# A hybrid layer with a streamed mixture of experts: gate chunks and query/key chunks change places, attention steps go between the branch products, the first gather goes between router pieces

## The chip, the cores and the metric

The kernel runs on one core of one Trainium2 chip. The metric is the device time in microseconds from launch to end; lower is better. TensorE (PE) does the matmuls and transposes, VectorE (DVE) and ScalarE (ACT) the elementwise work, SyncE (SP) issues nearly all loads, one after the other, on one queue.

## The reference

```python
def hybrid_layer(x, ...):                      # x: 256 tokens x 1024, float32
    proj = x @ w_in                            # 20 chunks of 256 columns and a low-rank part
    sh = token_shift(proj[..., :SHIFT_COLS], mu_shift)
    y_rwkv = rwkv7_time_mix(...)               # per head and token: state = state*w - (state@kk)(kk*a) + v k; y = state@r
    y_attn = moba_attention(q, k, v)           # rope on q and k; 256 tokens are one block: causal softmax attention
    mixed = (sigmoid(gate_a) * (y_attn @ w_attn_br)
             + sigmoid(gate_r) * (y_rwkv @ w_rwkv_br))
    h = layer_norm(DEEPNORM_ALPHA * x + mixed @ w_out, ln1_g, ln1_b)
    return layer_norm(DEEPNORM_ALPHA * h + moe_ffn(h, ...), ln2_g, ln2_b)

def moe_ffn(x, ...):                           # router: top 4 of 32 experts per token
    # each token's 4 experts: clamped_swiglu(x @ w1[e] + b1[e]) @ w2[e] + b2[e], weighted and added
```

All is float32. A product of the projections, branches and w_out is computed as three fp32r matmuls of a high and a low part (hi·hi, hi·lo, lo·hi): lines L135 to L137 of the kernel.

## The kernel before

The program is written out in one long function, and each engine executes its instructions in the order in which the program makes them, waiting where an operand or a buffer is not ready.

*Projections.* `units()` is a generator: each step of it is one unit, three matmuls. A chunk of 256 columns is 16 units, 320 in all; `fill(n)` draws n units, `fill_to(n)` draws up to the n-th. They stand between the steps of the serial work, so that TensorE has something to do while the other engines work on the step before. Before its units, each chunk has a later chunk's weights cut into high and low parts (`split`: L128 on ScalarE, L129 on VectorE). After its units a chunk is finished: shift chunks on ScalarE and VectorE (L205, L206), query and key chunks by the rotation of `rope` on VectorE (L274, L277, L279), gate chunks by one sigmoid on ScalarE. The order is: shift chunks, values, gate A (4 chunks), queries and keys (4), gate R (4).

*Recurrence.* VectorE makes the operands (L382 to L410), TensorE the products of each of the 4 chunks of 64 tokens (L426), VectorE solves a triangular system (L484, L486), whose blocks go through DRAM. Then comes the chain c = 0..3: L573 (state times keys), L580, L588 (new state), L601 (output) on TensorE, each followed by VectorE (L574, L581, L595/L596, L605) and by a few units. `group_norm(tt)` (L545 to L552) follows every second c, and `group_norm_out(tt)` (transposes L558, then L561, L562) makes the recurrence's result.

*Attention.* Transposes of q and k (L629), then for both halves h of the heads `scores(h)` (L642, L648, softmax L651 to L661), `turn_scores(h)` (transposes L667), `weigh(h)` (L680, L681).

*Branches and out projection.* The two branch products have 4 quarter-chunks of 16 units each; the result, multiplied by the gates G_["R"] and G_["A"], is `mixed`. The out projection takes w_out in 8 rows kt: each is cast (L819, ScalarE) and its low part made (L820, VectorE), then multiplied. The first five rows are done for all of the output, the rest piece by piece, together with the LayerNorm, the transposes L858 and the router L866. w_out arrives in four pieces of 1 MB (`wout_raw` 25 to 28, two rows each).

*Experts.* 32 experts of 12.58 MB each are streamed through twelve 2 MB buffers, whose memory the front uses for other things: `both0` to `both6` are pairs of slots (`BOTH`), the others are q0 to q3 and a pair (11, 13). `mfill(u)` puts the next load into buffer u on SP's queue. In the traces SP's loads of experts are L736, of w_out L758. The first expert starts with L1045 (biases) and L1049. Its rows are gathered by matmuls with one-hot matrices (L912 on VectorE, `gather_rows` L917 on TensorE), for which the router's choice must be known (`route`, `places`).

Of the kernel before, what the change touches and what calls it, by code (L numbers as in the profile page):

```python
# [17 lines left out]
T = 256  # L18
# [44 lines left out]
def hybrid_kernel(ctx, tc, xt_d, x_d, win_d, w0_d, ups_d, up2_d, par_d, cA_d, cB_d, wbr_d, wout_d,  # L63
# [11 lines left out]

    BOTH = [(0, 1), (22, 23), (21, 25), (14, 17), (16, 20), (9, 15), (12, 18)]
    both = [slots.tile([128, 2, 2048], FT, name=f"both{i}", tag=f"both{i}") for i in range(len(BOTH))]
# [27 lines left out]

    chunks = [("low", 0)] + [("in", i) for r in ((0, 6), (10, 16), (6, 10), (16, 20)) for i in range(*r)]
    chunks += [("br", i) for i in (2, 3, 0, 1)]
    raw_of = {0: 25, 21: 10, 22: 8, 23: 16, 24: 20, 25: 12, 26: 18, 27: 12, 28: 18}
    hls = ["q0", "q1", "q3"]
# [141 lines left out]
    def units():  # L251
        yield from proj_shift(1, 0, k, 0, 4)
        yield from proj_shift(2, 1, k, 2, 6)
        yield from proj_shift(3, 0, r, 0, 0)
        yield from proj_shift(4, 1, r, 2, 2)
        yield from proj_shift(5, 0, v, 0, 8)
        yield from proj_shift(6, 1, v, 2, 10)

        for half in range(2):
            yield from proj_tok(7 + half, half,  # L260
                                lambda tt, ps: A.copy(va_tok[:, tt, 256 * half:256 * half + 256], ps))
        G_["A"] = slot(15, [8, T])
        for j in range(4):
            yield from proj_gate(9 + j, j % 2, G_["A"][:, 2 * j:2 * j + 2])
        qk = G_["qk"] = slot(22, [2, 2, 512])
        cosf = cB[:, B_COS:B_COS + 128].rearrange("p (t d) -> p t d", t=2)
        sinf = cB[:, B_SIN:B_SIN + 128].rearrange("p (t two d) -> p t two d", t=2, two=2)
        m1 = s23[:, 1536:1792].rearrange("p (h d) -> p h d", d=64)
        m2 = s23[:, 1792:2048].rearrange("p (h two d) -> p h two d", two=2, d=32)

        def rope(which, half):
            def done(tt, ps):
                pv = ps.rearrange("p (h two d) -> p h two d", two=2, d=32)
                V.tensor_tensor(m1, pv.rearrange("p h two d -> p h (two d)"),  # L274
                                cosf[:, tt, None].to_broadcast([128, 4, 64]), op=OP.mult)
                for x in range(2):
                    V.tensor_tensor(m2[:, :, x], pv[:, :, 1 - x], sinf[:, tt, None, x].to_broadcast([128, 4, 32]),  # L277
                                    op=OP.mult)
                V.tensor_tensor(qk[:, which, tt, 256 * half:256 * half + 256], m1.rearrange("p h d -> p (h d)"),  # L279
                                m2.rearrange("p h two d -> p (h two d)"), op=OP.add)  # L280
            return done

        for u in range(4):
            yield from proj_tok(13 + u, u % 2, rope(*divmod(u, 2)))
        G_["R"] = slot(9, [8, T])
        for j in range(4):
            yield from proj_gate(17 + j, j % 2, G_["R"][:, 2 * j:2 * j + 2])

# [87 lines left out]
    PE.matmul(pd, cA[0:1, A_ONE:A_ONE + 1].to_broadcast([1, 128]), brow, start=False, stop=True)  # L376
    fill_to(46)
    for f2 in range(2):
# [82 lines left out]
    PT = s23[:, 0:1536].rearrange("p (f q) -> p f q", f=4)  # L461
    fill(4)

# [100 lines left out]
    for c in range(4):  # L564
# [56 lines left out]
    V.tensor_tensor(yRs[:, 1], yR, yRs[:, 0].bitcast(FT), op=OP.subtract)  # L621
    fill(8)
    qk = G_["qk"]
    qkT = slot(20, [2, 4, T])
    for f in range(4):
# [4 lines left out]
        A.copy(qkT[:, :, f], ps)  # L630
    fill(4)
    yAs = slot(13, [2, 4, T], FR)
# [4 lines left out]
    def scores(h):  # L637
# [6 lines left out]
        for f2 in range(2):  # L644
            pq = bank((7, 2)[f2], (2, T))
            for ff in range(2):
# [119 lines left out]
    V.tensor_tensor(b1r[:, 1], b1s, b1r[:, 0].bitcast(FT), op=OP.subtract)  # L766
    for n in (25, 26):
        wout_raw(n)
    mfill(0, "q2")
    gA, gR = G_["A"], G_["R"]  # L770
    for br, (ys_, gt) in enumerate(((yRs, gR), (yAs, gA))):
        for cc in range(2):
            n = 21 + 2 * br + cc
            split(n + 2)
            if n == 22:
                xtok = slot(8, [2, D])
                nc.scalar.dma_start(xtok, x_d)
            if n == 23:
                mx = [slot(i, [2, 4, T], FR) for i in (11, 10)]
            for dd in range(2):  # L780
                d2 = 2 * cc + dd
                ps = bank(2 + d2, (2, T))
                for d in range(2):
                    for kt in range(4):
                        c0 = 256 * dd + 128 * d
                        mm3(ps[:, d], [HL[n][:, x, kt, c0:c0 + 128] for x in range(2)], (ys_[:, 0, kt], ys_[:, 1, kt]),
                            kt == 0, kt == 3)
                q = slice(2 * d2, 2 * d2 + 2)
                V.tensor_tensor(gt[:, q], gt[:, q], ps, op=OP.mult)
                if br:  # L790
# [3 lines left out]
                    V.tensor_tensor(m[:, 1, q4], gA[:, q], m[:, 0, q4].bitcast(FT), op=OP.subtract)  # L794
                elif cc == 0 and dd == 0:
                    turn_scores(1)
                elif cc == 0:
                    weigh(1)
                    mfill(3, 1, 2)
# [14 lines left out]
    for kt in range(8):  # L814
# [74 lines left out]


    for n in range(len(todo) + 2):
        if n < len(todo):
            add(*todo[n])
        if n > 1:
            router(*todo[n - 2])
            if n == 3:
                route(0)
        if 0 < n <= len(todo):
            rows_turned(*todo[n - 1])
    route(1)  # L900
    mfill(*[hls[n % 3] for n in (27, 28)])
    dump("lg", lg[:, :, 0:E])

    ext = slot(10, [2048])
    XG, oh = ext[:, 0:1024].rearrange("p (d s) -> p d s", d=8), ext[:, 1024:1280].rearrange("p (t s) -> p t s", t=2)
    rows = ext[32:48, 1280:1408]
    OT = misc.tile([128, 2, 256], FR, name="OT", tag="OT")
# [437 lines left out]
```

## Time and profile before

| | |
|---|---|
| median of 3 runs | 1201.11 us (1199.92 to 1202.76) |
| the profiled execution | 1202.04 us, its span 1200.3 us |
| TensorE busy | 1124.0 us, 94% of the span |
| VectorE, ScalarE busy | 384.2 us, 280.1 us |
| granted TensorE clock, mean | 0.973 of full speed |
| loaded | 441 MB, 367 GB/s over the span |

Times in the views are counted from the start of the span. The execution's own time is 1.7 us more than its span. A busy TensorE is not one at its peak: 64 columns of the array are used in most expert matmuls, and they may wait for weights inside.

### The profile page before, as it was taken

The numbers are of one execution on the slowest core, as the hardware profiler recorded it, in microseconds if no ns is written. First come the engines' busy times: TensorE is split into PE (matmuls) and PEld (weight loads), VectorE is DVE, ScalarE is ACT, GpSimd is POOL, SyncE is SP. The second block draws the span as 40 slices with busy tenths as digits, with TensorE's granted clock in tenths as the row PEclk, the third lists the DMA queues.
The fourth block names the chain that finished last, engine by engine and source line by source line (L and its number), as shares of the span: only waits on it lengthen the run. The fifth ranks groups of instructions, "written<-read, shape, count | busy, mean of one in ns | idle before, by whom it ended". The sixth has DMA issues, their size and how long they took to land. (4 is left out here: it accounts for less than half of the span.)

```text
span 1200.3 us, 15200 instructions
## 1 busy us (share of the span) xinstructions
PE 1124.0 (94%) x6434; PEld 590.3 (49%) x6434; DVE 384.2 (32%) x809; ACT 280.1 (23%) x566; POOL 6.1 (1%) x16
## 2 busy tenths in 40 slices
PE   8989979999999999999999998999999799899995
PEld 6879969985434444343434343433343333343432
DVE  4879576662222222222212121211212111111113
ACT  5634326632111121111111111111111111111112
POOL 0000000000000000000000000000000000000000
PEclk9999989998999999999999999998999899999998
DMA  8344553797999999999999999999999989999995
GB/s 278 127 137 135 152 206 137 324 382 279 428 428 427 428 427 428 427 426 422 426 428 428 428 428 428 428 427 428 427 428 428 420 344 428 427 427 428 428 428 239
DMA packets 45549, 441.02 MB, mean 367 GB/s; under 512 B 13010, under 2 KB 13538, under 8 KB 17954
## 3 DMA queue, kind: packets, MB, share of 16 engines
q1 hardware_dynamic: 36002, 436.93, 87.6%
q10 hardware_dynamic: 9472, 3.05, 1.0%
q8 instruction: 52, 0.85, 0.3%
q14 instruction: 23, 0.19, 0.0%
HBM read 438.13 MB, written 1.84 MB: 367 GB/s over the span
## 5 line engine op out<-in xcount | busy, mean ns | idle before, releaser
L1049 PE MATMUL b<-both,s 128*64 128x512 f32 x1456 | 331.9, 605 | 17.5 <-DMA both<-in_w_dram 17.4
L1049 PEld LDWEIGHTS b<-both,s 128*64 128x64 f32 x1456 | 100.8, 139 | 227.8 <-issue 190.7
L1058 DVE TENSOR_SCALAR s<-b 128x256 f32<-128x256 f32 x64 | 27.2, 424 | 446.9 <-PE b L1049 446.9
L1032 PE MATMUL b<-both,s 128*64 128x512 f32 x624 | 139.7, 595 | 4.0 <-DMA both<-in_w_dram 3.2
L1049 PE MATMUL b<-q,s 128*64 128x512 f32 x576 | 132.4, 606 | 1.6 <-DMA q<-in_w_dram 1.5
L135 PE MATMUL b<-q,q 128*128 128x256 f32 x320 | 96.6, 302 | 0.9 <-ACT q L128 0.9
L1074 ACT COPY s<-b 128x256 f32<-128x256 f32 x64 | 23.7, 370 | 312.0 <-PE b L1069 229.5
L137 PE MATMUL b<-q,q 128*128 128x256 f32 x320 | 92.9, 290 | 0.8 <-DVE q L129 0.8
L136 PE MATMUL b<-q,q 128*128 128x256 f32 x320 | 92.8, 290 | 0.0
L1032 PEld LDWEIGHTS b<-both,s 128*64 128x64 f32 x624 | 43.8, 137 | 86.5 <-issue 82.7
L1032 PE MATMUL b<-q,s 128*64 128x512 f32 x368 | 83.0, 597 | 0.9 <-DMA q<-in_w_dram 0.9
L1022 DVE TENSOR_TENSOR s<-b,s 64x512 fp32r<-64x512 f32 (+1 forms) x66 | 44.3, 672 | 119.2 <-ACT s L1021 117.0
L1021 ACT CAST s<-b 64x512 fp32r<-64x512 f32 (+1 forms) x66 | 37.4, 567 | 189.5 <-PE b L1032 177.8
L1049 PEld LDWEIGHTS b<-q,s 128*64 128x64 f32 x576 | 39.7, 139 | 81.6 <-issue 76.7
L917 PEld LDWEIGHTS b<-s,s 128*128 128x128 f32 x512 | 61.7, 200 | 13.8 <-issue 13.0
L917 PE MATMUL b<-s,s 128*128 128x128 f32 x512 | 65.0, 288 | 1.4 <-DVE rt L961 0.7
L135 PEld LDWEIGHTS b<-q,q 128*128 128x128 f32 x320 | 63.6, 199 | 5.2 <-issue 2.6
L137 PEld LDWEIGHTS b<-q,q 128*128 128x128 f32 x320 | 63.7, 199 | 1.0 <-DVE q L129 1.0
L136 PEld LDWEIGHTS b<-q,q 128*128 128x128 f32 x320 | 63.8, 199 | 0.2 <-issue 0.2
L1059 ACT ACTIVATE s<-s 128x256 f32<-128x256 f32 x64 | 26.9, 421 | 144.7 <-DVE s L1058 144.7
L129 DVE TENSOR_TENSOR q<-both,q 128x1024 fp32r<-128x1024 f32 x44 | 52.4, 1218 | 10.6 <-ACT q L128 10.6
L1045 PE MATMUL b<-b1r,pick 128*128 128x512 f32 x128 | 47.2, 451 | 8.2 <-DVEq L1166 8.2
(291 smaller groups left out, 1040.1 us busy)
## 6 DMA issues: line engine op xcount, KB each, us to landing
both<-in_w_dram SPq DMA_DIRECT2D x130, 2048.0 KB, 25.7
q<-in_w_dram SPq DMA_DIRECT2D x59, 2048.0 KB, 34.5
both<-in_win_dram SPq DMA_DIRECT2D x19, 1024.0 KB, 5.1
both<-in_wout_dram SPq DMA_DIRECT2D x4, 1024.0 KB, 7.0
both<-in_w2l_dram SPq DMA_DIRECT2D x7, 512.0 KB, 21.5
s<-in_wbr_dram SPq DMA_DIRECT2D x2, 1024.0 KB, 6.8
both<-in_wbr_dram SPq DMA_DIRECT2D x2, 1024.0 KB, 4.8
s<-in_w_dram SPq DMA_DIRECT2D x2, 1024.0 KB, 16.5
```

What stands on the lines that cost most here:

```text
L129: V.tensor_tensor(hl[:, 1, c], RAW[n][:, c], hl[:, 0, c].bitcast(FT), op=OP.subtract)
L135: PE.matmul(ps, lhs[0], rhs[0], start=first, stop=False)
L136: PE.matmul(ps, lhs[0], rhs[1], start=False, stop=False)
L137: PE.matmul(ps, lhs[1], rhs[0], start=False, stop=last)
L917: PE.matmul(pg[d // 4][:, d % 4], xtok[:, tt, 128 * d:128 * d + 128], oh[:, tt], start=tt == 0 and d % 4 == 0, stop=tt == 1 and d % 4 == 3)
L1021: A.copy(hi, ps)
L1022: V.tensor_tensor(lo, ps, hi.bitcast(FT), op=OP.subtract)
L1032: PE.matmul(ps[64 * n:64 * n + 64], aTs[e % 2][:, b, hf, 64 * g_:64 * g_ + 64], w[:, hf, 512 * n:512 * n + 512], start=ft == 0, stop=ft == 7)
L1045: PE.matmul(ps, pick, b1r[:, x], start=x == 0, stop=False)
L1049: PE.matmul(ps[64 * g_:64 * g_ + 64], XG[:, kt, 64 * j:64 * j + 64], w[:, kt % 2, 512 * g_:512 * g_ + 512], start=False, stop=kt == 7)
L1058: V.tensor_scalar(gl, pv[:, :, 0], 7.0, None, op0=OP.min)
L1059: A.activation(sw, gl, AF.Sigmoid, scale=1.702)
```

## The change

BOTH is paired anew: pairs 4 and 5 were slots (16, 20) and (9, 15) and are (16, 9) and (20, 15). The chunks' order becomes: gate A (4), gate R (3), queries and keys (4), gate R (the last). Fills change: 46 to 50, 72 to 78, 4 to 9, and in the chain 4 to 5; `group_norm_out(0)` goes behind the chain's last step. The branch products become a generator too, and the steps of attention stand between its units. `wout_raw(26)` goes into the branch, `mfill(5)` from behind piece 28 to ahead of piece 27. In the loop over the router's pieces, the first token half's places, one-hots and gather stand ahead of the last router piece. Lines move: L574, L580, L588 and L601 become L575 and so on, SP's L736 and L758 become L729 and L751, L558 becomes L559, L866 L870, L886/L887 L890/L891, L917 L904.

```diff
-    BOTH = [(0, 1), (22, 23), (21, 25), (14, 17), (16, 20), (9, 15), (12, 18)]
+    BOTH = [(0, 1), (22, 23), (21, 25), (14, 17), (16, 9), (20, 15), (12, 18)]
...
-    chunks = [("low", 0)] + [("in", i) for r in ((0, 6), (10, 16), (6, 10), (16, 20)) for i in range(*r)]
+    chunks = [("low", 0)] + [("in", i) for r in ((0, 6), (10, 19), (6, 10), (19, 20)) for i in range(*r)]
...
+        G_["R"] = slot(20, [8, T])
+        for j in range(3):
+            yield from proj_gate(13 + j, j % 2, G_["R"][:, 2 * j:2 * j + 2])
...
         for u in range(4):
-            yield from proj_tok(13 + u, u % 2, rope(*divmod(u, 2)))
-        G_["R"] = slot(9, [8, T])
-        for j in range(4):
-            yield from proj_gate(17 + j, j % 2, G_["R"][:, 2 * j:2 * j + 2])
+            yield from proj_tok(16 + u, 1 - u % 2, rope(*divmod(u, 2)))
+        yield from proj_gate(20, 1, G_["R"][:, 6:8])
...
-    fill_to(46)
+    fill_to(50)
...
-    fill_to(72)
+    fill_to(78)
...
-    fill(4)
+    fill(9)
...
         if c < 3:
-            fill(4)
-        if c == 2:
-            group_norm_out(0)
-    fill_to(256)
+            fill(5)
+    group_norm_out(0)
+    fill(14)
     group_norm_out(1)
...
-    fill(8)
+    fill_to(312)
...
-    fill(4)
+    fill_to(320)
...
     scores(0)
-    fill(18)
-    scores(1)
-    fill(12)
-    turn_scores(0)
-    fill_to(314)
-    weigh(0)
-    fill_to(320)
...
+    queue = branch(0)
+    fill(16)
+    scores(1)
+    mfill(4)
+    fill(8)
+    wout_raw(26)
+    xtok = slot(8, [2, D])
+    nc.scalar.dma_start(xtok, x_d)
+    turn_scores(0)
+    fill(4)
+    weigh(0)
+    turn_scores(1)
+    fill(2)
+    weigh(1)
+    fill(2)
+    mfill(3, 1, 2)
+    mx = [slot(i, [2, 4, T], FR) for i in (11, 10)]
+    queue = branch(1)
+    fill(32)
     dump("mixT", gA)
-    mfill(4)
+    mfill(5)
...
         if kt in (1, 3):
             wout_raw(27 + kt // 2)
-            if kt == 3:
-                mfill(5)
...
     for n in range(len(todo) + 2):
         if n < len(todo):
             add(*todo[n])
+        if n == len(todo) + 1:
+            pg = [bank(i, (4, 128)) for i in (2, 3)]
+            gather_rows(pg, 0)
         if n > 1:
             router(*todo[n - 2])
             if n == 3:
                 route(0)
+            if n == len(todo):
+                ...
+                places(0)
+                one_hots(0, 0)
         if 0 < n <= len(todo):
             rows_turned(*todo[n - 1])
     route(1)
...
-    places(0)
-    one_hots(0, 0)
-    gather_rows(pg, 0)
     places(1)
```

How the change moves instructions shows best at three places. The first is VectorE in the chain's second and third steps; before, it is this (L274, L277 and L279 are the rotation of a query or key chunk, L129 a chunk's split, L581 to L605 the chain's own):

```order
L574 TENSOR_TENSOR both_71<-b_119_1424,both_71 64x512
L274 TENSOR_TENSOR both_70<-b_111_1313,both_72 128x256
L277 TENSOR_TENSOR both_70<-b_111_1313,both_72 128x4x32 x2
L581 COPY both_73<-b_120_1448 64x512
L279 TENSOR_TENSOR both_70<-both_70 128x256
L129 TENSOR_TENSOR q_121_1458<-both_69,q_121_1458 128x1024
L274 TENSOR_TENSOR both_70<-b_111_1313,both_72 128x256
L277 TENSOR_TENSOR both_70<-b_111_1313,both_72 128x4x32 x2
L129 TENSOR_TENSOR q_121_1458<-both_69,q_121_1458 128x1024
L279 TENSOR_TENSOR both_70<-both_70 128x256
L595 TENSOR_TENSOR s_11_126<-b_124_1474,s_11_126 64x4x64 x2
L596 TENSOR_TENSOR s_11_126<-s_11_126,eC 64x4x64 x2
```

The same place of VectorE's order after the change (L575 is L574 of before, L596 and L597 are L595 and L596):

```order
L575 TENSOR_TENSOR both_71<-b_119_1420,both_71 64x512
L582 COPY both_73<-b_123_1444 64x512
L129 TENSOR_TENSOR q_120_1434<-both_69,q_120_1434 128x1024 x2
L596 TENSOR_TENSOR s_11_126<-b_124_1463,s_11_126 64x4x64 x2
L597 TENSOR_TENSOR s_11_126<-s_11_126,eC 64x4x64 x2
```

The two rotations (six rows) are gone from between the steps; the two splits stay.

The second place is SP's order around the branch's end; `both_74` is pair 5, `in_wout` are pieces 25 to 28 of w_out, in that order. Before:

```order
L736 DMA both_71<-in_w_dram 128x4096
L736 DMA both_73<-in_w_dram 128x4096
L758 DMA both_75<-in_wout_dram 128x2x1024 x2
L736 DMA both_74<-in_w_dram 128x4096
L736 DMA both_75<-in_w_dram 128x4096
```

After:

```order
L729 DMA both_73<-in_w_dram 128x4096
L751 DMA both_75<-in_wout_dram 128x2x1024
L729 DMA both_72<-in_w_dram 128x4096
L729 DMA both_70<-in_w_dram 128x4096
L729 DMA both_71<-in_w_dram 128x4096
L729 DMA both_74<-in_w_dram 128x4096
L751 DMA both_75<-in_wout_dram 128x2x1024 x2
L729 DMA q_202_2438<-in_w_dram 128x4096
L729 DMA both_75<-in_w_dram 128x4096
```

Pair 5 stood behind pieces 27 and 28, and now stands ahead of both.

The third place is TensorE at the end of the router, up to the first expert's biases. Before (L866 is the router, L858 the transposes for it, L917 a gather, L886 and L887 the places of a half):

```order
L866 MATMUL b_206_2448<-wr,zT 128x32 x2
L858 MATMUL b_211_2558<-cA,s_182_2161 128x128 x2
L866 MATMUL b_206_2448<-wr,zT 128x32 x2
L887 MATMUL b_205_2447<-rt,cA 128x32
L917 MATMUL b_215_2582<-s_214_2580,s_182_2161 128x128 x4
L917 MATMUL b_216_2583<-s_214_2580,s_182_2161 128x128 x4
L886 MATMUL b_206_2448<-rt,cA 128x32
L887 MATMUL b_206_2448<-rt,cA 128x32
```

After (L870 is the router, L862 its transposes, L904 the gather, L890 and L891 the places):

```order
L870 MATMUL b_206_2448<-wr,zT 128x32 x2
L891 MATMUL b_205_2447<-rt,cA 128x32
L862 MATMUL b_212_2563<-cA,s_173_2121 128x128 x2
L904 MATMUL b_213_2568<-s_211_2559,s_173_2121 128x128 x4
L904 MATMUL b_214_2569<-s_211_2559,s_173_2121 128x128 x4
L870 MATMUL b_206_2448<-wr,zT 128x32 x2
L890 MATMUL b_206_2448<-rt,cA 128x32
L891 MATMUL b_206_2448<-rt,cA 128x32
```

The first half's gather has moved from behind the last router piece to ahead of it.

## Rows read from the trace of the kernel before

**Rows 1.** Windows: length; busy (instructions) PE, PEld, DVE, ACT, POOL; clock, DMA share, GB/s

```profile
560.00:960.00 400.00, 369.12 (x1828) 150.04 (x1826) 79.42 (x186) 61.04 (x149) 0.00 (x0) 0.97 1.01 427
```

**Rows 2.** TensorE's timeline: start, us, instruction, idle time before it

```profile
273.36 3.78 PE L917 MATMUL b<-s,s 128*128 128x128 f32 x16 [0.61 <-DVE rt L876]
...
278.58 3.65 PE L917 MATMUL b<-s,s 128*128 128x128 f32 x16 [0.75 <-DVE rt L961]
...
282.37 0.73 PE L1045 MATMUL b<-b1r,pick 128*128 128x512 f32 x2
...
314.92 3.84 PE L917 MATMUL b<-s,s 128*128 128x128 f32 x32
```

**Rows 3.** TensorE's waits before 285 us: releaser, us, times, longest

```profile
PE b L558 <- DVE both L552: 3.4, 1, 3.4
PE b L580 <- DVE both L574: 3.1, 1, 3.1
PE b L426 <- DVE s L410: 2.2, 1, 2.2
PE b L468 <- DVE s L206: 1.6, 1, 1.6
PE b L573 <- DVE s L596: 1.5, 1, 1.5
PE b L382 <- DVE both L369: 1.4, 1, 1.4
PE b L558 <- issue: 1.3, 1, 1.3
```

**Rows 4.** Windows of the front, columns as in rows 1

```profile
46.90:54.00 7.10, 7.01 (x38) 6.50 (x39) 6.95 (x14) 2.57 (x6) 0.90 (x2) 0.76 0.09 36
62.20:68.00 5.80, 5.79 (x48) 5.09 (x50) 4.54 (x9) 0.00 (x0) 0.00 (x0) 0.71 0.62 195
...
150.70:159.80 9.10, 7.81 (x86) 7.26 (x87) 7.59 (x16) 4.37 (x6) 0.00 (x0) 1.00 0.23 95
165.40:173.00 7.60, 7.55 (x51) 7.09 (x52) 2.92 (x6) 0.58 (x1) 0.00 (x0) 0.55 0.86 301
178.70:184.00 5.30, 5.30 (x33) 5.30 (x33) 4.15 (x11) 1.05 (x1) 0.00 (x0) 0.68 0.61 198
...
269.10:282.40 13.30, 10.91 (x57) 10.01 (x56) 4.02 (x26) 4.35 (x8) 0.00 (x0) 0.62 0.99 419
```

**Rows 5.** TensorE's timeline: last branch units, the out projection's first and fifth row

```profile
235.77 0.28 PE L137 MATMUL b<-s,q 128*128 128x256 f32 x1
...
243.09 0.40 PE L135 MATMUL b<-q,s 128*128 128x512 f32 x1
...
254.21 0.40 PE L135 MATMUL b<-q,s 128*128 128x512 f32 x1
```

**Rows 6.** VectorE's timeline within the chain

```profile
147.36 1.20 DVE L129 TENSOR_TENSOR q<-both,q 128x1024 fp32r<-128x1024 f32 x1
148.49 0.41 DVE L279 TENSOR_TENSOR both<-both 128x256 f32<-128x256 f32 x1
148.82 0.86 DVE L595 TENSOR_TENSOR s<-b,s 64x256 f32<-64x256 f32 x2
```

**Rows 7.** SP's timeline: issues of pieces 27 and 28 (one row), of pair 5

```profile
235.24 7.91 SPq L758 DMA_DIRECT2D both<-in_wout_dram  x2
246.69 0.34 SPq L736 DMA_DIRECT2D both<-in_w_dram  x1
```

**Rows 8.** DMA issues near 203.6 and 255.8 us: KB, us to landing

```profile
both<-in_w_dram SPq DMA_DIRECT2D x1, 2048.0 KB, 9.3
...
both<-in_w_dram SPq DMA_DIRECT2D x1, 2048.0 KB, 7.5
```

**Rows 9.** ScalarE's timeline: casts of w_out's rows 4 and 5

```profile
249.81 2.00 ACT L819 CAST q<-both 128x1024 fp32r<-128x1024 f32 x2 [3.87 <-DMA both<-in_wout_dram]
```

**Rows 10.** VectorE's timeline: splits of w_out's rows 4 to 7

```profile
250.89 4.86 DVE L820 TENSOR_TENSOR q<-both,q 128x1024 fp32r<-128x1024 f32 x4 [4.23 <-ACT q L819]
```

More of the change, by code (lines that the diff above doesn't have):

```diff
@@ L101, in dump @@
             dbg(name, ap)
-    chunks = [("low", 0)] + [("in", i) for r in ((0, 6), (10, 16), (6, 10), (16, 20)) for i in range(*r)]
+    chunks = [("low", 0)] + [("in", i) for r in ((0, 6), (10, 19), (6, 10), (19, 20)) for i in range(*r)]
     chunks += [("br", i) for i in (2, 3, 0, 1)]
-    raw_of = {0: 25, 21: 10, 22: 8, 23: 16, 24: 20, 25: 12, 26: 18, 27: 12, 28: 18}
+    raw_of = {0: 25, 21: 10, 22: 8, 23: 16, 24: 18, 25: 12, 26: 18, 27: 12, 28: 18}
     hls = ["q0", "q1", "q3"]
@@ L621, in hybrid_kernel @@
     V.tensor_tensor(yRs[:, 1], yR, yRs[:, 0].bitcast(FT), op=OP.subtract)
-    fill(8)
+    fill_to(312)
     qk = G_["qk"]
-    qkT = slot(20, [2, 4, T])
+    qkT = slot(9, [2, 4, T])
     for f in range(4):
@@ L644, in scores @@
         for f2 in range(2):
-            pq = bank((7, 2)[f2], (2, T))
+            pq = bank((7, 0)[f2], (2, T))
             for ff in range(2):
@@ L664, in turn_scores @@
         for i in range(3):
-            ps = bank((6, 7, 2)[i], (4, 128))
+            ps = bank((0, 1, 6)[i], (4, 128))
             for f in range(4):
@@ L766, in hybrid_kernel, with branch @@
     V.tensor_tensor(b1r[:, 1], b1s, b1r[:, 0].bitcast(FT), op=OP.subtract)
-    for n in (25, 26):
-        wout_raw(n)
+    wout_raw(25)
     mfill(0, "q2")
     gA, gR = G_["A"], G_["R"]
-    for br, (ys_, gt) in enumerate(((yRs, gR), (yAs, gA))):
+    def branch(br):
+        ys_, gt = ((yRs, gR), (yAs, gA))[br]
         for cc in range(2):
@@ L774, in hybrid_kernel @@
             split(n + 2)
[L775 to L779, printed above, removed]
             for dd in range(2):
@@ L787, in hybrid_kernel @@
                             kt == 0, kt == 3)
+                        if d + kt < 4:
+                            yield
                 q = slice(2 * d2, 2 * d2 + 2)
@@ L794, in hybrid_kernel @@
                     V.tensor_tensor(m[:, 1, q4], gA[:, q], m[:, 0, q4].bitcast(FT), op=OP.subtract)
[L795 to L799, printed above, removed]
+                yield
+    queue = branch(0)
[17 more added lines that the diff above has]
+    fill(32)
     dump("mixT", gA)
-    mfill(4)
+    mfill(5)
     po = [bank(i) for i in (0, 1, 2, 3, 5)]
@@ L888, in places @@
         V.scalar_tensor_tensor(posm[:, tt], pp, 1.0, sel[:, tt], op0=OP.add, op1=OP.mult)
[L891 to L906, printed above, removed]
     OT = misc.tile([128, 2, 256], FR, name="OT", tag="OT")
@@ L935, in gather @@
         gathered(pg)
-    pg = [bank(i, (4, 128)) for i in (2, 3)]
-    places(0)
-    one_hots(0, 0)
-    gather_rows(pg, 0)
+    for n in range(len(todo) + 2):
+        if n < len(todo):
+            add(*todo[n])
+        if n == len(todo) + 1:
+            pg = [bank(i, (4, 128)) for i in (2, 3)]
+            gather_rows(pg, 0)
+        if n > 1:
+            router(*todo[n - 2])
+            if n == 3:
+                route(0)
+            if n == len(todo):
+                ext = slot(10, [2048])
+                XG, oh = ext[:, 0:1024].rearrange("p (d s) -> p d s", d=8), ext[:, 1024:1280].rearrange("p (t s) -> p t s", t=2)
+                rows = ext[32:48, 1280:1408]
+                places(0)
+                one_hots(0, 0)
+        if 0 < n <= len(todo):
+            rows_turned(*todo[n - 1])
+    route(1)
+    mfill(*[hls[n % 3] for n in (27, 28)])
+    dump("lg", lg[:, :, 0:E])
     places(1)
```

## The prediction

> **What bounds the kernel now.** I read the windows first. From 560 to 960 us the DMA share is 1.01 at 427 GB/s while TensorE is busy 369 of 400 us [rows 1]: the expert stage is paced by its weights. TensorE's timeline then gives the place at which that stage can start, the bias matmul L1045 of the first expert at 282.37 us [rows 2]; 1200.3 - 282.37 = 917.9 us come after it. Twelve 2 MB buffers are filled ahead, and each later load waits until TensorE has read its buffer, so the stream begins when TensorE enters the first expert. I therefore take the end as that entry plus 917.9 us, one for one. None of the change's edits lies behind the entry.
>
> What sets the entry is the front. Its waits on TensorE, listed by engine and releaser, are seven single ones of 1.3 to 3.4 us, and all but one wait for VectorE [rows 3]: L382 for a reciprocal, L426 for L410, L468 for L206, and four in or behind the recurrence's chain (L573, L558 for nothing visible, L580, L558 for L552). Behind most of them the granted clock is below 1 [rows 4]: 0.76 in the 7.1 us from 46.9, 0.71 in the 5.8 from 62.2, 0.55 in the 7.6 from 165.4, 0.68 in the 5.3 from 178.7. A stretch of T us at clock x does the work of T·x at 2.4 GHz, so T·(1-x) is lost: 1.70, 1.68, 3.42 and 1.70 us. TensorE executes the same matmuls before and after up to the last branch product, which ends where the out projection starts, 243.09 us before [rows 5]. So the lead there is idle time removed plus clock loss removed, less what is new.
>
> **The change part by part.** *Fills in the front* (46 to 50, 72 to 78, 4 to 9). A unit is three matmuls at 0.12 us (60 of them lie between 235.77 and 243.09 [rows 5], 7.32/61), so 0.36 us. Four units cover L382's wait of 1.4, six of 2.2 us stand ahead of L426; VectorE gets there about as much earlier as L382 does, so I leave 1.5 of that wait (0 to 2.2). Five units cover L468's 1.6. Removed: 1.4 + 0.7 + 1.6 = 3.7 us, and the clock loss of 1.70 behind 46.9. That behind 62.2 I count as removed and then, since a wait of 1.5 remains there, as kept. New: the six units are missing further on, behind the L426 products; six units are 2.2 us of cover, VectorE is itself earlier, and I take 1.7 (0 to 2.2).
>
> *Gates in place of queries and keys.* In the chain, VectorE's order has a query chunk's rotation and weight split between two updates of the state: L129 for 1.20 us and L279 for 0.41 end at 148.9, where L595 starts (148.82) [rows 6]; TensorE's L573 waits for what follows. A gate chunk ends in a sigmoid on ScalarE, busy for 0.58 of the 7.6 us from 165.4 [rows 4], so this VectorE work leaves the chain; moving group_norm_out(0) behind c = 3 takes L561 and L562 out of it too, and fill(5) adds 0.36 us of cover per step. Removed: 1.5 + 1.3 + 3.1 = 5.9 us of waits and 3.42 of clock loss. What remains of c = 3's latency I charge with 1.0 (0 to 2.2, six units' worth of shift). The rotations fall behind the chain: the second L558 waits for the same kind of work as before (3.4), now with one rotation and two splits ahead of it: 3.6, so 0.2 more (0 to 4), and its 1.70 of clock loss stays.
>
> *Attention between the branch's products.* Between scores(0) and turn_scores(0) there were 30 units, now 16 + 8: 2.2 us less cover for a softmax of unchanged length. I take 1.85 of it as wait, and 0.8 where the first transposes wait for the last rotation: 2.65 (0 to 4).
>
> *Sum at the end of the branch.* Waits 9.6 and clock 1.70 + 1.68 + 3.42 = 6.8 removed: 16.4. New 1.7 + 1.0 + 0.2 + 2.65 = 5.55, clock kept 1.7. Lead 9.15, so the out projection starts at 233.9.
>
> *Buffer pair 5 ahead of w_out's pieces 27 and 28.* This is the part that works against the rest. Before, SP issued piece 27 at 235.24, ahead of the branch's end, and pair 5 only at 246.69, when VectorE had read gate A for the last time: 3.6 us behind the branch's end at 243.09 [rows 5, 7]. Afterwards pair 5 holds the slots of both gates and stands in SP's order ahead of pieces 27 and 28. It still waits for that last read, and both pieces wait behind it. A 2 MB load into an empty or nearly empty queue landed 7.5 to 9.3 us after its issue [rows 8]; 1 MB behind it takes 1.05/427 = 2.45; then ScalarE's cast, 1.0 each [rows 9], and VectorE's split, 4.86/4 = 1.22 each [rows 10]. The fifth row of the out projection would be ready 3.6 + (7.5 to 9.3) + 2.45 + 1.0 + 1.22 = 15.8 to 17.6 us behind the branch's end. TensorE wants it after four rows: 254.21 - 243.09 = 11.1 [rows 5]. Stall 4.7 to 6.4; I take 5.5. ScalarE already waited 3.87 for such a piece before [rows 9], hidden by the rows in hand. Behind 28 the order is slack: a row takes TensorE 2.8, a split 1.22.
>
> The Trainium skill (DMA: Bandwidth & Descriptors, "Anatomy of one DMA") gives 2.0 us fixed and bytes at 436 GB/s. By that page pair 5 would land in an estimated 6.8 us, the stall would be 3.9 and the time about 1196.9. The rows of this case are slower than the page, and the sum goes by them.
>
> *What such a stall does to the clock.* Behind waits of 3.1 and 3.4 us the losses were 3.42 and 1.70 us [rows 3, 4]. Behind 5.5 I take 2.5 (0 to 3.4; 0 because the stretch from 150.7 to 159.8, behind a wait of 1.5, stayed at 1.00 [rows 4]).
>
> *The first gather between the router pieces.* From 269.10 to 282.40 the clock is 0.62, a loss of 5.1 us, and short waits lie in it. The first gather takes 3.78 us from 273.36, the second 3.65 from 278.58, where 32 of the same at 2.4 GHz take 3.84 [rows 2, 4]: 1.9 for 16. Placed ahead of the last router piece, the first gather covers the copy for it, but uncovers the top-4 selection on VectorE behind that piece, which lay under it. If the clock holds, the stretch shrinks by up to 3.5 us, if not by nothing; I take 1.5, between the two.
>
> **Sum.** 9.15 - 5.5 - 2.5 + 1.5 = 2.65 us earlier. The profiled execution took 1202.04 with a span of 1200.3; its 917.9 behind the entry are unchanged, so its counterpart is 1199.4. The median of the three runs is 1201.11, 0.9 below the profiled one; from it I forecast 1198.5.
>
> **Rivals.** *The stall is small and the clock holds.* If piece 27 arrived in time (pair 5 free earlier than the last product, or its load over sooner), the front's lead would come through: 9.15 + 1.5 to 3.5, so 1188.5 to 1190.5. Against it: both slots of the pair are gates, which the last product reads. Chance 0.18; half a stall lies between, near 1195.
>
> *Slower: VectorE is late at the second L558.* Eight splits and four rotations now lie behind the chain, on the path to attention. If that wait is 8 us instead of 3.6, the lead at the branch's end is 4.8, and 5.5 + 2.5 - 1.5 = 6.5 eats it: 1202.8, or 1204.6 with the longest stall and the longest loss. It decides from a lead under 6.5. For it: every named wait of the chain is VectorE's [rows 3]. Against it: the second L558 has 14 units ahead of it. Chance 0.18.
>
> *It does nothing to the end.* The preloads, which the same stall delays, could still be under way when TensorE enters the first expert. Then the DMA queue, and not the entry, sets the stream, which before was already at 0.99 of its time in the last 13 us [rows 4], and a lead of any size ends within 2 us of 1201. Against it: pairs 0 to 4 now start about as much earlier as TensorE does. Chance 0.14.
>
> **How the numbers follow.** The forecast has the rest, 0.5. Its own range is 1193.5 (stall 4.7, loss 1.7, gather 3.5, lead 10.5) to 1203 (lead 7.5, stall 6.4, loss 3.4, gather 0). Leaving out the full success at its low end and the worst of the slower case gives 1190.5 to 1203.5 for 8 in 10. 0.2%, about what a measurement can tell from no change, is 2.4 us: faster means under 1198.7, slower over 1203.5. The forecast falls just inside the first: 0.3 of its 0.5 are faster, 0.17 the same, 0.03 slower. The first rival is all faster, the second 0.04 same and 0.14 slower, the third 0.04 faster, 0.09 same and 0.01 slower. Together 0.52, 0.30, 0.18.
>
> **What would show it.** Right: no wait over 1 us in the chain, clock 1.00 from there to the second L558; the branch ends near 234; a single wait of TensorE of about 5 us in the out projection, on the split of row 4, with pair 5's issue ahead of piece 27's; the clock under 1 right behind it. Wrong: piece 27 landed before TensorE's fourth row ends; a wait over 5 us at the second L558 or in attention; an entry into the first expert whose shift doesn't come back at the end.

## The result, and the profile after

The changed kernel takes 1209.47 us (median of 5 runs, 1206.78 to 1210.23) against 1201.64 of the kernel before (5 runs); the ratio is 1.0071, interval 1.0055 to 1.0086: slower by 0.7%, where 1198.5 and a range up to 1203.5 were forecast. The profiled execution has a span of 1207.7 us, 7.4 more than before.

TensorE's timeline of the changed kernel has the places that matter: the first products behind the triangular solve, the start of the out projection, its fifth row, and the entry into the first expert.

```profile
128.38 0.69 PE L522 MATMUL b<-s,s 32*32 32x32 f32 x16 [1.40 <-DMA s<-tblk]
...
245.25 0.40 PE L135 MATMUL b<-q,s 128*128 128x512 f32 x1
...
260.59 0.80 PE L135 MATMUL b<-q,s 128*128 128x512 f32 x1 [4.06 <-ACT q L825]
...
289.24 0.99 PE L1051 MATMUL b<-b1r,pick 128*128 128x512 f32 x2
```

The entry is at 289.24 where it was at 282.37 [rows 2]: 6.9 us later, and the span is longer by about as much (7.4). Behind the entry the windows read as before [rows 1]:

```profile
560.00:960.00 400.00, 371.98 (x1830) 151.94 (x1828) 80.39 (x188) 61.97 (x150) 0.00 (x0) 0.96 1.01 427
```

So the loss lies in the front. The out projection starts at 245.25 instead of 243.09 [rows 5]; there was no lead at all to lose. Which waits are left is in the list of TensorE's waits from 100 to 292 us:

```profile
PE b L135 <- ACT q L825: 4.1, 1, 4.1
PE b L559 <- DVE both L553: 3.3, 1, 3.3
PE b L522 <- DMA s<-tblk: 1.4, 1, 1.4
PE b L667 <- DVE both L660: 1.2, 1, 1.2
```

The waits of 1.5, 1.3 and 3.1 us within the chain [rows 3] are gone. In their place stand the forecast one in the out projection (L135) and one that the forecast did not have, L522's for a DMA. What it is worth shows in the windows behind it and behind the out projection's stall:

```profile
128.30:147.00 18.70, 18.58 (x208) 17.38 (x209) 6.26 (x7) 7.32 (x10) 0.00 (x0) 0.54 0.48 136
245.20:260.00 14.80, 11.33 (x62) 9.63 (x61) 3.05 (x5) 1.75 (x3) 0.00 (x0) 0.97 0.71 279
260.00:270.00 10.00, 8.95 (x31) 7.06 (x32) 6.03 (x7) 3.48 (x4) 0.00 (x0) 0.70 0.93 363
```

From 128.3 to 147 us TensorE is busy for 18.6 of 18.7 us at a granted clock of 0.54: nearly all of it at 1.2 GHz. That is 18.7 x 0.46 = 8.6 us of work lost, more than the whole result, behind a wait of 1.4 us. Before, the clock from 150.7 to 159.8 was 1.00 behind a wait of 1.5 [rows 3, 4].

Why L522 waits is read on VectorE, SP and ScalarE. VectorE's timeline at the end of the triangular solve (L485 and L487 are its steps, L501 makes the transposed copy, both results go to DRAM and come back as blocks):

```profile
117.36 0.21 DVE L485 TENSOR_TENSOR both<-both 64x60 f32<-64x60 f32 x1
117.50 2.35 DVE L129 TENSOR_TENSOR q<-both,q 128x1024 fp32r<-128x1024 f32 x2
119.78 0.21 DVE L487 TENSOR_TENSOR both<-both,both 64x60 f32<-64x60 f32 x1
...
120.45 1.11 DVE L501 COPY both<-both 64x1024 f32<-64x1024 f32 x1
```

A weight split of 2.35 us stands inside the solve, two steps from its end. There it is a sixth one: the five units more ahead of L469 bring the next chunk's start forward by five units, and VectorE's order puts its split ahead of the last steps. When the split is done, SP issues the next chunk's 1 MB load, and ScalarE issues the write to DRAM right after it (SP's and ScalarE's timelines, and the DMA view of the write: KB, us to landing):

```profile
119.88 0.33 SPq L119 DMA_DIRECT2D both<-in_win_dram  x1
```

```profile
120.50 0.50 ACTq L503 DMA_DIRECT2D tblk<-both  x1
...
126.44 4.10 ACTq L512 DMA_DIRECT2D s<-tblk  x8
```

```profile
tblk<-both ACTq DMA_DIRECT2D x1, 256.0 KB, 5.9
```

The first of the two writes of 256 KB takes 5.9 us; the load ahead of it takes 5.9 us too, so that it is under way until 125.8. The eight reads are issued only behind this write, from 126.44 to 130.5. TensorE has drawn its 208 units at 126.98 and waits.

### The profile page after: what moved, and what is told of

It is laid out like the page before. It is cut to its first block, busy times and chain, and to the rows that moved or that the text cites. A ratio compares the mean times of both kernels' runs of the same rounds, so it can differ in the third digit from the quotient of the medians.

```text
span 1207.7 us, 15201 instructions
## 1 busy us (share of the span) xinstructions
PE 1135.7 (94%) x6434; PEld 597.4 (49%) x6434; DVE 383.1 (32%) x809; ACT 280.0 (23%) x565; POOL 6.1 (1%) x16
## 5 line engine op out<-in xcount | busy, mean ns | idle before, releaser
L135 PE MATMUL b<-q,q 128*128 128x256 f32 x320 | 97.7, 305 | 0.9 <-ACT q L128 0.9
L137 PE MATMUL b<-q,q 128*128 128x256 f32 x320 | 94.2, 294 | 0.8 <-DVE q L129 0.8
L136 PE MATMUL b<-q,q 128*128 128x256 f32 x320 | 94.3, 295 | 0.0
L135 PEld LDWEIGHTS b<-q,q 128*128 128x128 f32 x320 | 65.0, 203 | 4.2 <-issue 1.6
L904 PEld LDWEIGHTS b<-s,s 128*128 128x128 f32 x512 | 59.5, 195 | 13.5 <-issue 13.0
L137 PEld LDWEIGHTS b<-q,q 128*128 128x128 f32 x320 | 65.2, 204 | 1.0 <-DVE q L129 1.0
L136 PEld LDWEIGHTS b<-q,q 128*128 128x128 f32 x320 | 65.2, 204 | 0.2 <-issue 0.2
L904 PE MATMUL b<-s,s 128*128 128x128 f32 x512 | 62.8, 282 | 1.1 <-DVE rt L964 0.7
L129 DVE TENSOR_TENSOR q<-both,q 128x1024 fp32r<-128x1024 f32 x44 | 52.5, 1218 | 18.8 <-ACT q L128 18.7
## 6 DMA issues: line engine op xcount, KB each, us to landing
both<-in_wout_dram SPq DMA_DIRECT2D x4, 1024.0 KB, 10.4
```

What stands on the lines that cost most here:

```text
L129: V.tensor_tensor(hl[:, 1, c], RAW[n][:, c], hl[:, 0, c].bitcast(FT), op=OP.subtract)
L135: PE.matmul(ps, lhs[0], rhs[0], start=first, stop=False)
L136: PE.matmul(ps, lhs[0], rhs[1], start=False, stop=False)
L137: PE.matmul(ps, lhs[1], rhs[0], start=False, stop=last)
L904: PE.matmul(pg[d // 4][:, d % 4], xtok[:, tt, 128 * d:128 * d + 128], oh[:, tt], start=tt == 0 and d % 4 == 0, stop=tt == 1 and d % 4 == 3)
```

## The experiments

Theory A: the round trip of the triangular solve through DRAM ends too late for a TensorE that comes early; TensorE's wait for it takes the clock down for 17 us, and the queue's order in the out projection adds a stall of 4.5 us and a clock loss of its own. Theory B: the clock falls in the chain's first products for another reason (their narrow matmuls, the phase in which they meet it), whatever TensorE waits for. The first four kernels undo one part of the change each, or two.

**e1_fill4.** One number put back.

```diff
-    fill(9)
+    fill(4)
```

> The changed kernel with one number put back: 4 units instead of 9 ahead of the transposes L469. Theory A (the sixth weight split of VectorE inside the triangular solve makes the DRAM round trip late; TensorE's 1.40 us wait for it at L522 is what drops the clock from 129 to 147 us): the sixth split falls behind the solve, the solve ends near 118 us instead of 120.4, no wait at L522, clock 1.00 from 120 to 147, the first expert starts 8 to 10 us earlier than in the changed kernel (289.24), at 279.5 to 282, time 1199 to 1202, ratio to the kernel before 0.998 to 1.000. Theory B (the clock falls there because the narrow matmuls L522 and L530 meet it in a bad phase, wait or not): only the 1.4 us come back, clock near 0.54 from 129 to 147 as in the changed kernel, time near 1208, ratio 1.006.

Measured: 1201.68, ratio 1.0012 (0.9997 to 1.0026). The split stands behind the solve, which ends 2.3 us earlier in this execution (e3 shows that this is hardly the split's doing), and the write takes 3.5 us. VectorE's timeline of e1_fill4, and its DMA view of the write:

```profile
117.97 0.18 DVE L487 TENSOR_TENSOR both<-both,both 64x31 f32<-64x31 f32 x1
118.19 1.13 DVE L501 COPY both<-both 64x1024 f32<-64x1024 f32 x1
119.25 2.34 DVE L129 TENSOR_TENSOR q<-both,q 128x1024 fp32r<-128x1024 f32 x2
```

```profile
tblk<-both ACTq DMA_DIRECT2D x1, 256.0 KB, 3.5
```

TensorE's first products there and the window behind them, of e1_fill4:

```profile
128.59 0.69 PE L522 MATMUL b<-s,s 32*32 32x32 f32 x16
```

```profile
128.30:147.00 18.70, 18.70 (x293) 17.61 (x292) 9.44 (x11) 10.31 (x14) 0.00 (x0) 1.00 0.37 120
```

No wait, and the same products at 1.00. L522 itself starts no earlier than in the changed kernel (128.38): the 1.4 us did not come back, the 8.6 did. The entry is at 280.15, 9.1 us earlier. This is what theory A said (the ratio a little above its 0.998 to 1.000), and against B. TensorE comes later here, since it loses 1.8 us at L469 and some clock there; that it does not wait is in part this.

**e2_pieces_first.** Pair 5 behind pieces 27 and 28 again.

```diff
     dump("mixT", gA)
-    mfill(5)
...
         if kt in (1, 3):
             wout_raw(27 + kt // 2)
+            if kt == 3:
+                mfill(5)
```

> The changed kernel with buffer pair 5 loaded behind pieces 27 and 28 of w_out again, as before the change. Theory A (the stall of 4.06 + 0.46 us in the out projection is the queue's order, and the clock loss of about 3.4 us between 245 and 270 us follows from it): no wait in the out projection, clock 1.00 there, the first expert 7 to 8 us earlier, time near 1201.5, ratio 0.999 to 1.002, while the 17 us at half clock from 129 us stay. Rival (the stall costs only itself, because the clock would fall at the router's short waits anyway): 4.5 us earlier, time near 1205, ratio 1.003.

Measured: 1199.51, ratio 0.9992 (0.9978 to 1.0007). No wait in the out projection, clock 1.00; the window from 245 to 270 of e2_pieces_first, and its wait at L522:

```profile
245.00:270.00 25.00, 24.48 (x151) 21.54 (x150) 13.42 (x30) 9.56 (x13) 0.00 (x0) 1.00 0.94 379
```

```profile
126.19 0.69 PE L522 MATMUL b<-s,s 32*32 32x32 f32 x16 [1.57 <-DMA s<-tblk]
```

The entry is at 279.47, 9.8 us earlier than in the changed kernel. 2.2 of these arise ahead of L522 (126.19 against 128.38), where this execution lost almost no clock; 7.6 are the stall and the clock behind it. The wait at L522 and 0.58 from 128.3 to 147 stayed.

**e3_both_back.** Both of these edits at once.

> The changed kernel with both put back: 4 units ahead of L469 and pair 5 behind pieces 27 and 28. If the two losses are separate and both causes are right they add: the first expert 15 to 18 us earlier than 289.24, at 271 to 274, time 1192 to 1194.5, ratio 0.992 to 0.994. If the clock falls at other places instead: 1197 to 1202.

Measured: 1193.72, ratio 0.9953 (0.9934 to 0.9971), entry at 272.55, 16.7 us earlier than in the changed kernel; time and entry are as expected, the ratio is above the expected 0.992 to 0.994. The two losses add, 9.1 of e1 and 7.6 of e2, as separate causes do. Without them the change is faster by 0.5%.

e2 and e3 together also tell which part of the sixth split makes the blocks late. With the split inside, e2's solve ends at 118.05; with the split behind it, e3's ends at 117.95. The writes that follow at once differ: in e2 SP has issued a 1 MB load at 117.51, 0.6 us ahead of the write; in e3 the last load ahead of the write is from 115.68, 2.4 us ahead, and the next one comes behind it, at 121.42. The DMA views of the write, of e2_pieces_first and of e3_both_back:

```profile
tblk<-both ACTq DMA_DIRECT2D x1, 256.0 KB, 6.1
```

```profile
tblk<-both ACTq DMA_DIRECT2D x1, 256.0 KB, 3.2
```

So it is the load that the split brings with it, and not the split's own 2.35 us.

**e4_gather_back.** `places(0)`, `one_hots(0, 0)` and `gather_rows(pg, 0)` back behind `route(1)`, all else as changed.

> The changed kernel with the first gather back behind the last router piece. From the transposes L862 of the fourth piece to the first expert it took 13.2 us in the kernel before and 10.7 in the changed one. If the edit is worth this difference: 2.5 us later than the changed kernel, time near 1212, ratio 1.009. If the 10.7 come from a better clock behind the stall instead and not from the place of the gather: within 1 us of the changed kernel, ratio 1.006 to 1.008.

Measured: 1206.6, ratio 1.0056 (1.0035 to 1.0076). Not slower than the changed kernel, so the first reading fails; what the place of the gather is worth is asked again in e12.

**e5_cover.** More units ahead of L522, the late write left as it is.

```diff
-    fill_to(208)
+    fill_to(216)
```

> The changed kernel with 8 more units drawn ahead of L522 (up to the 216th instead of the 208th; they are missing later). The sixth split and the slow DRAM write stay. Theory A (TensorE's wait at L522 is what drops the clock): no wait at L522, clock 1.00 from 128 to 147 us, the first expert 8 to 10 us earlier than in the changed kernel, time 1199 to 1202, ratio 0.998 to 1.001. Theory B (the clock falls in this stage because of the narrow matmuls, or because of the slow write's traffic): the wait is gone but the clock stays near 0.55 there, time near 1207.5, ratio 1.005 to 1.007.

Measured: 1208.4, ratio 1.0063 (1.0048 to 1.0078). By its total this looks like theory B. It is not, as TensorE's timeline of e5_cover shows:

```profile
127.45 0.69 PE L522 MATMUL b<-s,s 32*32 32x32 f32 x16
...
133.31 3.23 PE L530 MATMUL b<-s,both 32*32 32x32 f32 x64 [2.48 <-issue]
```

The wait was not removed but moved: L522 starts without one and runs at full speed, and 2.48 us are waited ahead of L530. The clock falls behind that wait (0.65 from 136 to 147). The narrow matmuls alone, L522, did not take it down. The units were missing later: the second L559 waited 4.8 instead of 3.3. Neither theory's expectation had the second wait.

**e6_units_between.** The wait at L522 kept, more units behind it.

```diff
         A.copy(Xs[hi], px[pr][hi])
-    fill(3)
+    fill(8)
...
     dump("Um", Um)
-    fill(3)
+    fill(8)
```

> The changed kernel with 8 units instead of 3 behind the L522 products and again behind the L530 products (they are missing later). The wait at L522 stays, 1.4 to 2.4 us. If the narrow matmuls (32 x 32, then 64 x 64) are what holds the clock down for 17 us once it has fallen: it is back at 1.00 after the first or second run of units, the low stretch is 3 to 8 us long, time 1202 to 1205, ratio 1.000 to 1.004. If the stretch lasts as long whatever runs in it: 17 us at about 0.5 again, time near 1207.5, ratio 1.005 to 1.007.

Measured: 1207.32, ratio 1.0046 (1.0034 to 1.0059). Windows of e6_units_between, and its L530 products:

```profile
128.00:136.00 8.00, 7.98 (x88) 7.80 (x87) 3.47 (x3) 5.63 (x7) 0.00 (x0) 0.57 0.51 101
136.00:147.00 11.00, 11.00 (x162) 10.43 (x161) 5.15 (x7) 4.21 (x6) 0.00 (x0) 1.00 0.49 167
```

```profile
136.13 2.11 PE L530 MATMUL b<-s,both 32*32 32x32 f32 x64
```

The clock is back at the end of the eight units, after some 7 us instead of 17, and the L530 products take 2.11 us (3.4 at the lower clock). So how long the clock stayed down here depended on what TensorE ran meanwhile: some 17 us with three units behind each of the two groups of narrow matmuls, some 7 with eight. The total shows nothing of it; the chain lacked ten units later: new waits of 2.4 and 2.6 us for VectorE, and clock 0.80 from 160 to 176.

**e7_fills_alone.** The kernel before, with the three front fills of the change and nothing else.

```diff
-    fill_to(46)
+    fill_to(50)
...
-    fill_to(72)
+    fill_to(78)
...
-    fill(4)
+    fill(9)
```

> The kernel before with the three front fills of the change alone (50, 78 and 9 in place of 46, 72 and 4). Theory A: the sixth split goes into the triangular solve here too, the write to DRAM takes 6 us instead of 3.7, TensorE waits 1 to 2.5 us at L522 and the clock is near 0.55 for some 17 us behind it; the 3.7 us gained further ahead are outweighed: time 1203 to 1207, ratio 1.002 to 1.006. If the fills do what the forecast took them for: 3 to 4 us earlier, ratio 0.996 to 0.998.

Measured: 1202.79, ratio 1.0012 (1.0002 to 1.0023). The mechanism is there, in the kernel before; TensorE's timeline and window of e7_fills_alone:

```profile
126.55 0.69 PE L521 MATMUL b<-s,s 32*32 32x32 f32 x16 [1.34 <-DMA s<-tblk]
...
128.06 0.93 PE L521 MATMUL b<-s,s 32*32 32x32 f32 x16 [0.31 <-DMA s<-tblk]
```

```profile
128.00:147.00 19.00, 18.94 (x189) 17.91 (x190) 6.26 (x7) 6.87 (x9) 0.00 (x0) 0.55 0.42 126
```

L521 starts 2.7 us earlier than before (129.21), so the fills did gain in front, and the clock takes 19 x 0.45 = 8.6 back. A part of that returns in the chain, where the low clock cost 5.1 us before [rows 4] and 15 x 0.23 = 3.4 here (0.77 from 172 to 187). The price in total, 0.1%, came out under the one that I had set.

**e8_fill24.** e3_both_back, with more cover at the second L559.

```diff
     group_norm_out(0)
-    fill(14)
+    fill(24)
     group_norm_out(1)
```

> The version with both put back (4 units ahead of L469, pair 5 behind pieces 27 and 28), and 24 units instead of 14 ahead of the second L559 (they are missing behind it). If the 3.3 us wait there is only missing cover: it goes, the first expert starts 3 to 5 us earlier than that version's 272.55, time 1189 to 1191, ratio 0.991 to 0.993. If the splits and rotations that come with the extra units delay L553 as much as they cover: wait of 2 us or more, time 1193 to 1195, ratio 0.994 to 0.996.

Measured: 1190.49, ratio 0.9906 (0.9892 to 0.9921): the fastest version here. The wait of 3.3 us at L559 is gone, and the clock from 176 to 200, 0.93 in the changed kernel, is 1.00. The profiled execution, at 1194.07 the longest of four, does not show the gain at the entry (274.52, where 3 to 5 us less than 272.55 were expected): its clock was 0.51 from 32 to 39 us, where e3's was 1.00; it came to L522 4.2 us later than e3's and needed 2.3 us less from there. TensorE's longest waits left between 100 and 275 us in e8_fill24:

```profile
PE b L629 <- DVE both L282: 1.4, 1, 1.4
PE b L667 <- DVE both L660: 1.2, 1, 1.2
PE b L135 <- DVE both L280: 0.9, 1, 0.9
```

**e9_load_later.** What makes the round trip late, the split's own time or the load that follows it? The split stays in the solve, the load waits until the first block is back.

```diff
-        load(n + 2)
+        if n != 14:
+            load(n + 2)
...
+    late1 = misc.tile([128, 1], FT, name="late1")
+    V.tensor_tensor(late1[64:65], RAW[14][64:65, 0:1], Tm[64:65, 0, 0, 0:1], op=OP.add)
+    load(16)
     fill_to(208)
```

> The changed kernel, with the 1 MB weight load that follows the sixth split held back until the first block has come back from DRAM (one addition of one element by VectorE reads that block and the split's source, and the load waits for it). The sixth split stays inside the triangular solve, 9 units stay ahead of L469. Theory A2 (what makes the round trip late is that this load runs into the write to DRAM): the write takes 3 to 4.5 us instead of 5.9, no wait or one under 0.5 us at L522, clock 1.00 from 128 to 147 us, time 1199 to 1202, ratio 0.998 to 1.001. Rival (the split's own 2.35 us inside the solve are what is late): the write gets shorter but the wait stays over 1 us and the clock falls for some 17 us, time near 1207, ratio 1.004 to 1.006.

Measured: 1204.56, ratio 1.0039 (1.0024 to 1.0054). The DMA view of the write in e9_load_later, ScalarE's timeline, and TensorE's (L526 and L534 are L522 and L530, L527 the copy behind L526):

```profile
tblk<-both ACTq DMA_DIRECT2D x1, 256.0 KB, 2.9
```

```profile
122.70 5.68 ACTq L513 DMA_DIRECT2D s<-tblk  x8
128.43 1.99 ACT L128 CAST q<-both 128x1024 fp32r<-128x1024 f32 x2 [7.28 <-DMA s<-tblk]
...
130.94 1.18 ACT L527 COPY both<-b 32x512 f32<-32x512 f32 x2
```

```profile
126.20 0.69 PE L526 MATMUL b<-s,s 32*32 32x32 f32 x16
...
132.15 3.40 PE L534 MATMUL b<-s,both 32*32 32x32 f32 x64 [2.58 <-ACT both L527]
```

Half of A2 holds: the write takes 2.9 us without the load and 5.9 with it, and TensorE no longer waits at L526. But it waits 2.58 us at L534, for which two things come late. ScalarE issues the reads until 128.4, then casts weights for 2 us, and only then copies L526's result; the first of its two copies ends near 131.5. And the load, issued at 124.97, now runs into the later reads, as the DMA view of e9_load_later shows (issues from 124.8 to 125.5):

```profile
both<-in_win_dram SPq DMA_DIRECT2D x1, 1024.0 KB, 6.7
s<-tblk ACTq DMA_DIRECT2D x2, 64.0 KB, 6.9
```

These reads, the second of which L534 needs too, land at 131.8 and 132.0, and L534 starts at 132.15. The profile names the copy, but the reads ended last. The clock is 0.63 behind it. So a TensorE that is at L526 by 126.2 is too early for both. The time lies between the two expectations. The eight executions spread from 1202.79 to 1207.6, and the profiled one took 1207.58; what happened at L534 in the shortest is not known.

**e10_all.** The changed kernel with e2's order, 24 units as in e8 and the late load of e9, 9 units as changed.

> The changed kernel with pair 5 behind pieces 27 and 28, 24 units ahead of the second L559, 9 units ahead of L469 as changed, and the weight load held back as in e9. If A2 holds, it has the gains of the version with 24 units (1190.49) and no 1.8 us wait at L469: the first expert at 271 to 274, time 1188 to 1191, ratio 0.989 to 0.992. If the wait at L522 comes back with 9 units: 1197 to 1200, ratio 0.996 to 0.999.

Measured: 1194.44, ratio 0.9951 (0.9934 to 0.9968). The second case: TensorE waits 1.9 us at L534, clock 0.63 from 128.3 to 147. The wait is for the reads that were issued behind the late load. Nine units ahead of L469 are worse than four, even with a short write.

**e11_pair5_first.** The kernel before, with pair 5 ahead of pieces 27 and 28 and nothing else.

```diff
     mfill(4)
+    mfill(5)
...
-            if kt == 3:
-                mfill(5)
```

> The kernel before with one edit of the change alone: pair 5 is loaded ahead of pieces 27 and 28 of w_out. Theory A (queue order makes the stall, and the stall takes the clock down): a wait of 4 to 5.5 us at the out projection's fifth row, clock under 0.9 from there to 270 us, the first expert 6 to 8 us later than 282.37, time 1207 to 1209, ratio 1.005 to 1.007. Rival (hidden, as piece 27 was issued late before too): wait under 1 us, ratio under 1.002.

Measured: 1209.2, ratio 1.0072 (1.0054 to 1.009). TensorE's waits from 240 to 285 us and the window of e11_pair5_first:

```profile
PE b L135 <- ACT q L820: 3.8, 1, 3.8
```

```profile
245.00:270.00 25.00, 20.76 (x95) 17.11 (x95) 8.39 (x12) 4.60 (x5) 0.00 (x0) 0.86 0.85 335
```

One line moved in one queue costs as much as the whole change: 3.8 + 0.5 us of stall, 25 x 0.14 = 3.5 us of clock.

**e12_gather_clean.** e3_both_back with the gather back, as in e4.

> The version with both put back (e3_both_back), and with the first gather back behind the last router piece too: what the gather's place is worth where nothing else disturbs it. By the stretch from the fourth router piece to the first expert (9.4 us there, 11.0 with the gather back in the changed kernel): 1.6 us later than e3_both_back, time near 1195.3, ratio 0.996 to 0.998. If its place is worth nothing: ratio near 0.995.

Measured: 1193.74, ratio 0.9945 (0.9927 to 0.9964), against 0.9953 (0.9934 to 0.9971) of e3_both_back. From the fourth router piece to the entry the profiles say 10.99 us here (266.49 to 277.48) and 9.40 there (263.15 to 272.55), so the stretch is 1.6 us shorter with the gather moved. The windows of e12_gather_clean and of e3_both_back say where that comes from:

```profile
266.49:277.48 10.99, 9.11 (x53) 8.37 (x53) 3.40 (x24) 3.93 (x7) 0.00 (x0) 0.69 1.00 427
```

```profile
263.15:272.55 9.40, 7.41 (x53) 6.53 (x53) 3.62 (x24) 3.97 (x7) 0.00 (x0) 0.89 1.03 438
```

The clock cost 10.99 x 0.31 = 3.4 us with the gather back and 9.40 x 0.11 = 1.0 with it moved: the clock is more than the whole difference. The times don't show it, and intervals of 0.18% to each side can't exclude it. What the place of the gather is worth in the end stays open.

## Why the prediction was wrong

**Its first step, that the entry decides, was right.** 6.9 us there are 7.4 at the end; the third rival (nothing at the end) is out.

**The step that failed is the lead into the chain.** Ahead of L522 the sum has a net lead of 3.7 us, and lets it go on through L522 at 129.2 - 3.7 = 125.5. TensorE was nearly there: ready at 126.98 in the changed kernel, whose execution lost 1.7 us to the clock from 46 to 58, and at 124.62 in e2, whose execution did not. But L522 reads the blocks that come back from DRAM, and these follow VectorE's solve, not TensorE. Before, TensorE came to them without a wait, and I took that for slack. At the next products, L529, there was some 0.5 us of it, as ScalarE's and TensorE's timelines of the kernel before show:

```profile
129.33 1.99 ACT L128 CAST q<-both 128x1024 fp32r<-128x1024 f32 x2 [5.17 <-DMA s<-tblk]
131.34 1.18 ACT L522 COPY both<-b 32x512 f32<-32x512 f32 x2
```

```profile
132.50 2.11 PE L529 MATMUL b<-s,both 32*32 32x32 f32 x64
```

ScalarE issues the reads until 129.3, casts weights and then makes the two copies, the first of which ends near 131.9; L529 reads it at 132.50. In none of the kernels with nine units could the lead pass: they waited 1.3 to 2.6 us at L522 or, with more cover or a faster write, at L530 (e5, e9, e10). And the edit that made TensorE early made the blocks late: it put the sixth split, and with it a 1 MB load, ahead of the write, and the load slows the write (e3, e9). VectorE's order showed the split ahead of the solve's last steps before anything ran. I had followed VectorE only where the split stood between chain steps.

**What that wait does was not in the sum at all.** I had priced a new clock loss only behind the stall in the out projection, and had taken the stretch from 150.7, at 1.00 behind a wait of 1.5 us, as the reason why a wait may cost no clock. Behind L522's 1.40 the loss is 8.6 us; at L522 itself it is 2.9 (128.4 for 125.5). A late split was among my rivals, with its place 50 us further on, at the second L558, where the wait stayed at 3.3 as forecast (3.6).

**The chain was right.** Its waits and its low clock are gone. From L522 to the second L558 it was 49.5 us before (129.21 to 178.70) and is 43.6 in e1 (128.59 to 172.18), with eight units more drawn in it, 2.9 us: 8.8 gained, where 5.9 + 3.42 - 1.0 - 0.2 = 8.1 were forecast. Attention too: 0.62 + 1.20 + 0.51 = 2.3 us of waits for 2.65.

**The stall in the out projection was right in place and cause, and nearly in size.** 4.06 + 0.46 = 4.5 us, where 5.5 were taken out of 4.7 to 6.4. SP issued pair 5 at 249.05, 3.8 us behind the branch's end, and both pieces right behind it; ScalarE's cast waited 11.19 us for the first:

```profile
249.05 0.33 SPq L729 DMA_DIRECT2D both<-in_w_dram  x1
249.43 0.95 SPq L751 DMA_DIRECT2D both<-in_wout_dram  x2
```

```profile
259.49 1.99 ACT L825 CAST q<-both 128x1024 fp32r<-128x1024 f32 x2 [11.19 <-DMA both<-in_wout_dram]
```

From pair 5's issue to the piece it is 10.4 us, within the 9.95 to 11.75 of the rows' sum (7.5 to 9.3, and 2.45). The Trainium skill's fit (DMA: Bandwidth & Descriptors, "Anatomy of one DMA"), 2.0 us and bytes at 436 GB/s, gives an estimated 9.2 for the 3.1 MB. The page states it for transfers issued from GpSimd, which the prediction left out, and these are SyncE's; the measurement decides. The clock behind cost 14.8 x 0.03 + 10 x 0.30 = 3.4 us, 2.5 forecast. e2 and e11 show that the line of SP's order is the cause, in both kernels.

**The gather** gave 2.5 us in the stretch (12.3 before, from 270.08; 9.8 after), where 1.5 were taken. The clock there cost 5.1 us before [rows 4] and 9.76 x 0.14 = 1.4 after, so the gain is the clock's, which the forecast had only at the upper end of this term (3.5). What of it is the gather's place is not settled (e12).

Added up as the forecast was: a lead of -2.2 where 9.15 were forecast, less 4.5 of stall, less 3.4 of clock, and 2.5 from the gather's stretch make 7.6 us later, and the entry was 6.9 later. e3, without the wait at L522 and without the stall, has 0.5% of gain.

## What to carry to other kernels

Where TensorE is given more work ahead of a point, ask what it reads there and which engine's chain that ends: if it came without a wait before, another path may end at the same moment, and a lead can't pass it. Look in every in-order engine for what the extra work brings forward, its loads too: here five units moved a split into the solve and a 1 MB load in front of a 256 KB write. And price a wait by the clock behind it as well as by its length: the best version here (e8) is the change with three waits taken out: L522's, the out projection's and the second L559's.

## What the runs showed of the hardware

All eight profiles with a wait of 1.3 to 2.6 us at L522 or L530 show 1.2 GHz behind it, for some 7 us (e6) to some 17: 0.54 to 0.63 from 128.3 to 147 in six of them, 0.73 and 0.82 in the two that had more units near (e5, e6). The six profiles without one (before, e1, e3, e8, e11, e12) show 1.00. The Trainium skill (TensorE: Matmul & The Clock Gate, "HAM oscillation") describes waits for DMA after which the next matmuls start at the lower clock. This trace agrees in kind, but the waits in the page's example, some 3 to 5 us, are longer than those here. That the clock then stays low for 17 us of nearly full occupation, and for 7 with longer runs of units (e6), I had not expected.

A wait doesn't always do this: L469's 1.8 us in e1, over at 82.1, was followed by the lower clock (0.66 from 82 to 87), L573's 1.5 before was not (1.00 from 150.7 to 159.8). In the front, executions differ: from 46 to 58 us the clock was 0.86 in the changed kernel, e1 and e6, and 1.00 in e2 to e5, with the same instructions up to there; what decides it is open.

Small transfers that were issued while a 1 MB load of another queue was under way landed only when that load was over. In the changed kernel the load was over at 125.8 and the write, issued 0.6 us behind the load, at 126.4; in e2 123.5 and 124.2; in e9 131.7 for the load and 131.8 and 132.0 for two of the reads, issued within 0.4 us of it. In e3 the load ahead of the write was over at 120.6 (issued at 115.68, 4.9 us), the write at 121.2. With no such load in the way, the write took 2.9 us (e9) and the reads 2.2 to 2.4 (e9's first three, the changed kernel's).
